# Three kept square sums on TensorE, two row slots, a second accumulator for the modulation columns, and another PSUM order: one change to a two-layer hybrid kernel

## The chip, the cores and the metric

The kernel runs on one core of one Trainium2 chip. The metric is device time in microseconds (us) of one execution. Engines are called by the names of the profile: PE (TensorE matmul), PEld (its weight load), DVE (VectorE), ACT (ScalarE), POOL (GpSimd), SP (SyncE, which here only issues DMAs).

## The reference, cut to what matters

Two layers run over 640 tokens (128 of a prompt, 512 of a sample) of width 1024. Each layer is a mixer and a SwiGLU FFN, each behind an RMSNorm whose scale and shift ("modulation") are products of two condition vectors with a large matrix:

```
mod  = silu(cond) @ ada_w[l] + ada_b[l]          # two conds (prompt, sample), 1024 x 6144 per layer
h    = rmsnorm(x, norm_mix_g[l]) * (1 + sc) + sh
x    = x + g * mixer_l(h)       # l=0: 4 mLSTM heads and 4 HGRN2 heads; l=1: differential attention, 8 heads
h    = rmsnorm(x, norm_ffn_g[l]) * (1 + sc2) + sh2
x    = x + g2 * (silu(h @ w1[l]) * (h @ w3[l])) @ w2[l]
y    = rmsnorm(x, final_norm_g)                  # behind the second layer
```

`rmsnorm` needs, of each token, the sum of 1024 squares. The mLSTM is chunkwise: of each head and each chunk of 128 tokens a 128x128 decay matrix (forward and backward) is made of row and column values, exponentiated and multiplied into the scores. The second layer's attention has a scalar `lam` made from `od_lambda`.

## The kernel before, in words

x lies feature-major, [128, 8, 640]: 8 blocks of 128 features, 640 tokens in the free dimension, worked in two halves a=0 and a=1 of 320 columns. Every fp32 product is three matmuls over split operands (high x high, low x high, high x low), all recorded at L188; transposes are at L193. Weights are loaded as 128x1024 fp32 (`raw`), and split into `wh` (ACT L318) and `wl` (DVE L319).

Order: a scheduler with its own timeline orders the instructions of ACT, DVE, POOL and SP; the order of PE is pinned as written in the mixers and in the transitions.

**Mixer of layer 0.** Eight units u (4 mLSTM heads `ml_mix`, u=0..3, then 4 HGRN2 heads `hg_mix`, u=4..7, `H4` = 4) run one after the other; a pacer (`Fill`) pulls the weight projections of the next unit into the steps of the present one. Beside them run side generators. In u=0..3 these are four units of `ada_vec` (L477 on): each makes 512 columns of modulation values without PE. It takes an accumulator `acc` (tag `qp`, one buffer), then 8 times loads a 128x512 piece `araw` (256 KB, two buffers in tag `fb`), scales it on ACT once for each of the two conditions (L486, into `acc` the first time, into `atmp` afterwards) and adds it on POOL (L488); at the end 4 PE matmuls `pj<-acc,ones` sum over the partitions. `add_side(..., 1)` lets one unit be loaded ahead of the unit that is being finished, and at `u == H4` a loop forces all that is left:

```
        if u == H4:
            while fill.side:
                fill.step_side()
```

In `ml_mix` each chunk makes `dm` = min(`nb`, `caus`) on DVE (L960), exponentiates it on ACT (L964), multiplies it with the scores and so on; `nb` holds rows of `nmd` from DRAM, broadcast to all partitions by `rows_of` (SP), in 5 slots of tag `kr`, loaded one head ahead.

**Transitions.** `transition()` stands three times: layer 0 mixer to FFN (T1), layer 0 FFN to attention (T2), attention to the last FFN (T3). Each adds the last products to x (`add_x`, DVE L371, 8 blocks of half 0, then of half 1), and has for each half: `sq_sum` (ACT L530 squares 8 blocks; 5 adds at L532 gather blocks 0 to 5 in `sq`, on POOL for half 0 and on DVE for half 1; DVE adds block 7 to block 6 at L534 and this to `sq` at L535), `columns` (5 matmuls `mean,sq` that put the means into 5 columns of 64 rows; DVE r L598; POOL power -0.5 L599; DVE dg L601), and `spread` (2 matmuls `dg,ones` that broadcast the result). Behind that, `norm_out` makes hh and hl on DVE and ACT (L548 to L570) and the next projection starts. Where in PE's order columns and spread stand is set by the tables BEFORE and BEHIND. In T2 the kernel also loads `lp` (`od_lambda`, SP L1590) and makes `nl` from it: DVE l2 L1593, DVE ls L1595, ACT exp L1596, DVE nl L1598.

**PSUM.** Pools of 8 banks are opened anew at each stage. `to_odd` opens one with tags pj, s and p1 for the second mixer, in place of a pool with pj (6 banks) and nm (2); a tag gets its banks when it is first used.

Of the kernel before, what the change touches and what calls it, by code (L numbers as in the profile page):

```python
# [9 lines left out]
F32 = mybir.dt.float32  # L10
F32R = mybir.dt.float32r
AF = mybir.ActivationFunctionType
ALU = mybir.AluOpType
# [3 lines left out]
P = 128  # L17
D = 1024
KD = D // P
NS = 512  # L20
NT = P + NS
NCH = NT // P
# [142 lines left out]
def hybrid_kernel(ctx: ExitStack, tc: tile.TileContext, A: dict, O: dict):  # L165
# [357 lines left out]
    def sq_sum(pool, a):  # L523

        t = slice(a * HALF, (a + 1) * HALF)
        sq = pool.tile([P, HALF], F32, tag="nsq", name="sq", bufs=2)
        s2 = pool.tile([P, HALF], F32, tag="ns2", name="s2", bufs=1)
        for k in range(KD):
            dst = {0: sq, SQUARES: s2}.get(k) or pool.tile([P, HALF], F32, tag="ns1", name="s1", bufs=2)
            S.activation(dst, x[:, k, t], AF.Square)  # L530
            if 0 < k < SQUARES:
                (V if a else G).tensor_tensor(sq, sq, dst, op=ALU.add)  # L532
            elif k > SQUARES:
                V.tensor_tensor(s2, s2, dst, op=ALU.add)  # L534
        V.tensor_tensor(sq, sq, s2, op=ALU.add)  # L535
        return sq

    def norm_out(pool, l, which, a, rs, ks=range(KD), keep=None):

# [44 lines left out]
    def transition(l, which, add, tag0, switch, tag1, nada, ada_bank, extra=0):  # L584
# [7 lines left out]
        def columns(sq, tag):  # L592

            o = bank(tag)
            for i in range(NC64):
                T.matmul(o[0:64, i:i + 1], lhsT=sq[:, i * 64:(i + 1) * 64], rhs=mean1, start=True, stop=True)
            r = pool.tile([64, NC64], F32, tag="nr", name="r", bufs=2)
            V.tensor_scalar(r, o[0:64, 0:NC64], EPS, None, op0=ALU.add)  # L598
            G.tensor_tensor(r, r, mhalf[0:64, 0:NC64], op=ALU.pow)  # L599
            dg = pool.tile([64, NC64, 64], F32, tag="ndg", name="dg", bufs=1)  # L600
            V.tensor_tensor(dg, ident[0:64, 0:64].unsqueeze(1).to_broadcast([64, NC64, 64]),  # L601
                            r.unsqueeze(2).to_broadcast([64, NC64, 64]), op=ALU.mult)
            return dg
# [306 lines left out]

        return (q, kf, so), [w_proj(c_q + h * P, evac_q), w_proj(c_k + h * P, evac_k), gen]

    nb = ev.tile([P, NCH, 2, P], F32, tag="kr", name="nb", bufs=1)

    def rows_of(h, c):

        Q.dma_start(nb[:, c], nmd[h, c:c + 1].to_broadcast([P, 2, P]))

    def ml_mix(h, q, kf, so):

# [34 lines left out]
        def weights(c):  # L955
            t = slice(c * P, (c + 1) * P)
            ps = p1()
            T.matmul(ps[:, 0:P], lhsT=kf[:, t], rhs=q[:, t], start=True, stop=True)
            dm = ev.tile([P, 2, P], F32, tag="dm", name="dm", bufs=2)
            V.tensor_tensor(dm, nb[:, c], caus, op=ALU.min)  # L960
            if h + 1 < H4:
                rows_of(h + 1, c)
            for r in range(2):
                S.activation(dm[:, r], dm[:, r], AF.Exp, bias=cols1[:, c, r, h:h + 1])  # L964
            V.tensor_tensor(dm, dm, ps[:, 0:P].unsqueeze(1).to_broadcast([P, 2, P]), op=ALU.mult)
            return dm
# [44 lines left out]

        mix["last"] = last

    for c in range(NCH):
        rows_of(0, c)


    def hg_bounds():
# [202 lines left out]
    for u, (_, mixer, h) in enumerate(units):  # L1221
        cur = nxt
        for p in HG_VALUES[u]:
            for g in hg_values(p):
                fill.add(g)
                val = g
        if u + 1 < len(units):
            nxt, gens = units[u + 1][0](units[u + 1][2])
            for g in gens:
                fill.add(g)  # L1230
        if u:
            fill.drain(key)
        key = gens[-1]
        for i in ADDS[u]:
            fill.add(add_gen(i))
        total = (48 * len(gens) if u + 1 < len(units) else 0) + 94 * len(HG_VALUES[u]) + 96 * len(ADDS[u])
        total += 48 if u == 0 else 0
        if u == 0:
            def acc():
                return ev.tile([P, 2, NT], F32, tag="qp", name="acc", bufs=1)[:, :, 0:512]  # L1240

            def raw():
                return ev.tile([P, NT], F32, tag="fb", name="araw", bufs=2)[:, 0:512]

            def tmp():
                return ev.tile([P, NT], F32, tag="kc", name="atmp", bufs=2)[:, 0:512]

            fill.add_side([ada_vec_gen(*i, raw, tmp, acc) for i in vec_units(VEC0)], VEC_EVERY, 1, eager=False)
        if u == H4:
            while fill.side:  # L1250
                fill.step_side()
        n, todo = ADA_UNITS[u], ada_todo[:ADA_UNITS[u]]
        del ada_todo[:n]
        if n:
            fill.add_side([ada_gen(j) for j in todo], total / (n + 0.5 - (2 if u == 7 else 0)))
        if u == 0:
            fill.pull(FILL0)
            total -= FILL0 * total / (total + 9 * n)
        quota = FRACTION[u] * (total + 9 * n) / (10 if u < H4 else 16)
        for step, w in enumerate(mixer(h, *cur)):  # L1260
            if u == H4 and step == len(LEVELS) + 1:
                fill.drain(val)
            fill.pull(w * quota)
            if last and step == LAST_STEP[u >= H4]:
                last()
                last = None
        last = mix["last"]
        if u == 3:
            ps = p1()
            T.transpose(ps[0:8, 0:P], nout.rearrange("p r h -> p (r h)"), ident)  # L1270
            nrow = ev.tile([8, P], F32, name="nrow")
            V.tensor_copy(nrow, ps[0:8, 0:P])
            Q.dma_start(O["mlstm_n"][0, 0].rearrange("r h d -> (r h) d"), nrow)
# [271 lines left out]
    def to_odd(behind):  # L1545
        ff["st"]["wide"].release()
        ff["st"]["pool"].release()
        psum["p"].release()
        psum_pool(pj=2, s=2, p1=2)
        ff["od"] = tc.alloc_tile_pool(name="od", bufs=1, reuse_waits="tile")  # L1550
        qk[0] = at_tiles()
        ws = [w_cols(w_in1, j * D, "r") for j in range(2)]
        with tc.issue_after(behind):
            wv = w_cols(w_in1, 2 * D)
        ff["vt"] = vt_tile()

        def first(a, between):
            os, t = proj_open(ws, a, between)
            for j in range(2):
                at_evac(j, qk[0][j], a, os[j], t)  # L1560
            (o,), t = proj_open([wv], a, lambda k: between(k + KD), [bank("s", 2)[:, 0:HALF]])
            S.copy(ff["vt"][:, t], o)

        return first
# [262 lines left out]
    def to_output():  # L1827
        ff["st"]["wide"].release()
        with tc.tile_pool(name="fi", bufs=1, reuse_waits="tile") as fi:
# [13 lines left out]
            def chunk(c):  # L1843
                o = bank("nm")
                for a in range(2):
                    t0, t1 = max(c * P, a * HALF), min((c + 1) * P, (a + 1) * HALF)
                    if t0 < t1:
                        T.matmul(o[t0 - c * P:t1 - c * P, 0:1], lhsT=sqs[a][:, t0 - a * HALF:t1 - a * HALF],
                                 rhs=mean1, start=True, stop=True)
                V.tensor_scalar(rcol[:, c:c + 1], o[:, 0:1], EPS, None, op0=ALU.add)  # L1850
                G.tensor_tensor(rcol[:, c:c + 1], rcol[:, c:c + 1], mhalf[:, 0:1], op=ALU.pow)
                for b in range(2):
# [58 lines left out]
```

## Time and profile before

| | us |
|---|---|
| median of 3 runs (lowest, highest) | 1824.48 (1822.47, 1824.6) |
| the profiled execution's own time | 1827.93 |
| its span in the trace | 1826.1 |
| PE busy in it | 1739.6 |

PE is busy 95% of the span, and its mean granted clock is 0.983 of full speed. Times of the trace run from the span's start; 1.8 us of the profiled execution lie outside the span. The mLSTM units of the first mixer lie at about 85 to 250 us, T1 at 487 to 515, T2 at 978 to 1015, T3 at 1355 to 1372, and the final norm behind 1806.

### The profile page before, as it was taken

How to read it: one execution, taken by the hardware profiler on the slowest of the kernel's cores; microseconds unless marked ns; L12 is line 12 of the kernel's file. 1: busy time of each engine (PE TensorE's matmuls, PEld its weight loads, DVE VectorE, ACT ScalarE, POOL GpSimd, SP SyncE). 2: the span in 40 equal slices, each digit the busy share in tenths (PEclk: the TensorE clock that was granted, in tenths of full speed). 3: DMA queues.
4: the chain of work that ended last, by engine and by line, in shares of the span. 5: the costliest groups of instructions: out<-in, count | busy, mean ns of one | idle time of the engine just before them, and what ended most of it. 6: DMA issues, size and time to landing. Idle time of an engine off the chain costs nothing.

```text
span 1826.1 us, 31627 instructions
## 1 busy us (share of the span) xinstructions
PE 1739.6 (95%) x12198; PEld 1661.5 (91%) x12198; DVE 1379.0 (76%) x2806; ACT 805.2 (44%) x1677; POOL 493.5 (27%) x409
## 2 busy tenths in 40 slices
PE   7998979999889999999999899999989999999998
PEld 5798969999778999999998898999978999999998
DVE  5657766677797777777778687777879887888787
ACT  5466543343353333333324466566536332333334
POOL 2244443233122222223211221112121333232321
PEclk9999989999989999999999999999999999999999
DMA  9344222122615434443412221112031322222211
GB/s 310 116 133 133 82 79 58 53 75 66 208 50 162 125 120 137 137 141 116 128 58 81 67 86 44 31 54 76 24 121 58 93 79 84 82 81 76 87 59 59
DMA packets 187979, 174.80 MB, mean 96 GB/s; under 512 B 7762, under 2 KB 168372, under 8 KB 187828
## 3 DMA queue, kind: packets, MB, share of 16 engines
q1 hardware_dynamic: 186564, 172.63, 30.7%
q8 instruction: 97, 1.59, 0.4%
q14 instruction: 54, 0.44, 0.1%
q10 hardware_dynamic: 1264, 0.14, 0.1%
HBM read 167.99 MB, written 4.74 MB: 95 GB/s over the span
## 4 chain that ended last, share of the span: by engine, by line
PE 76%; DVE 12%; DMA 4%; ACT 4%; issue 3%; POOL 1%; SPq 1%; ACTq 0%; DVEq 0%; POOLq 0%
PE pj L188 59%; PE nm L188 8%; PE p L188 5%; PE s L188 2%; DMA araw<-in_ada_w_dram 2%; DVE wl L319 2%; PE p L193 1%; DVE x L371 1%; ACT wh L318 1%; ACT atmp L486 1%; DVE hl L570 1%; DMA raw<-in_ffn_w_dram 1%; DMA wg<-in_ev_w_in_dram 0%; DVE hh L564 0%; PE pj L193 0%
## 5 line engine op out<-in xcount | busy, mean ns | idle before, releaser
L188 PE MATMUL pj<-hh,wh 128*128 128x320 f32 x1648 | 526.6, 322 | 11.9 <-DVE hh L564 5.7
L188 PE MATMUL pj<-hh,wl 128*128 128x320 f32 x1648 | 513.7, 312 | 0.0
L188 PE MATMUL pj<-hl,wh 128*128 128x320 f32 x1648 | 502.6, 313 | 2.1 <-DVE hl L570 1.9
L188 PEld LDWEIGHTS pj<-hh,wh 128*128 128x128 f32 x1648 | 313.1, 190 | 27.0 <-DVE hh L564 9.4
L188 PEld LDWEIGHTS pj<-hl,wh 128*128 128x128 f32 x1648 | 310.5, 190 | 3.9 <-DVE hl L570 2.4
L188 PEld LDWEIGHTS pj<-hh,wl 128*128 128x128 f32 x1648 | 313.8, 190 | 0.0
L188 PE MATMUL pj<-t,wh 128*128 128x320 f32 x960 | 217.0, 311 | 0.2 <-ACT wh L1322 0.2
L318 ACT CAST wh<-raw 128x1024 fp32r<-128x1024 f32 x127 | 132.6, 1048 | 184.8 <-PE pj L188 88.1
L319 DVE TENSOR_TENSOR wl<-raw,wh 128x1024 fp32r<-128x1024 f32 x127 | 162.8, 1284 | 40.0 <-ACT wh L318 39.7
L188 PEld LDWEIGHTS pj<-t,wh 128*128 128x128 f32 x960 | 160.9, 188 | 3.4 <-DVE o L1374 0.8
L1322 ACT CAST wh<-s 128x1024 fp32r<-128x1024 f32 x80 | 84.1, 1051 | 151.7 <-PE pj L188 151.7
L188 PE MATMUL pj<-t,wl 128*128 128x320 f32 x480 | 148.9, 310 | 1.1 <-DVE wl L1323 1.1
L1336 POOL TENSOR_TENSOR s<-raw 128x512 f32<-128x512 f32 x40 | 55.9, 1397 | 333.1 <-DVE wl L1323 331.5
L371 DVE SCALAR_TENSOR_TENSOR x<-nm,g2h,x 128x128 f32<-128x128 f32 (+1 forms) x236 | 93.5, 429 | 48.7 <-PE nm L188 48.3
L188 PE MATMUL pj<-ah,wh 128*128 128x320 f32 x392 | 122.5, 313 | 0.0
L188 PE MATMUL pj<-al,wh 128*128 128x320 f32 x392 | 121.3, 310 | 0.0
L188 PE MATMUL pj<-ah,wl 128*128 128x320 f32 x392 | 121.2, 309 | 0.0
L371 DVE SCALAR_TENSOR_TENSOR x<-pj,g2h,x 128x128 f32<-128x128 f32 (+2 forms) x292 | 112.1, 430 | 12.0 <-PE pj L188 11.3
L1338 POOL TENSOR_TENSOR s<-s,raw 128x512 f32<-128x512 f32 x40 | 66.4, 1659 | 198.3 <-DVE wl L1323 198.3
L1323 DVE TENSOR_TENSOR wl<-s,wh 128x1024 fp32r<-128x1024 f32 x80 | 97.2, 1215 | 8.5 <-ACT wh L1322 8.4
L1322 ACT CAST wh<-raw 128x512 fp32r<-128x512 f32 (+1 forms) x81 | 67.9, 838 | 80.1 <-PE pj L188 80.0
L188 PE MATMUL nm<-al,wh 128*128 128x320 f32 x312 | 96.3, 311 | 1.6 <-DVE al L1438 1.6
(415 smaller groups left out, 3898.4 us busy)
## 6 DMA issues: line engine op xcount, KB each, us to landing
raw<-in_ffn_w_dram SPq DMA_DIRECT2D x132, 512.0 KB
own<-in_ada_w_dram SPq DMA_DIRECT2D x48, 512.0 KB
raw<-in_ev_w_in_dram SPq DMA_DIRECT2D x36, 512.0 KB
raw<-in_od_w_in_dram SPq DMA_DIRECT2D x24, 512.0 KB
raw<-in_ada_w_dram SPq DMA_DIRECT2D x20, 512.0 KB
araw<-in_ada_w_dram SPq DMA_DIRECT2D x32, 256.0 KB
araw<-in_ada_w_dram SPq DMA_DIRECT2D x12, 512.0 KB
raw<-in_ev_w_out_dram SPq DMA_DIRECT2D x8, 512.0 KB
```

The source lines that it names most:

```text
L188: ins = nc.tensor.matmul(*args, **kw)
L193: ins = nc.tensor.transpose(*args, **kw)
L318: S.copy(wh, raw3)
L319: V.tensor_tensor(wl, raw3, wh.bitcast(F32), op=ALU.subtract)
L371: V.scalar_tensor_tensor(x[:, m, t0:t1], o[:, t0 - a * HALF:t1 - a * HALF], gate[:, m, c:c + 1], x[:, m, t0:t1], op0=ALU.mult, op1=ALU.add)
L486: S.activation(t, r, AF.Copy, scale=cpad[:, k, c:c + 1])
L570: order(V.tensor_tensor(hl[:, k, t], tmps[k], hh[:, k, t].bitcast(F32), op=ALU.subtract))
L1322: S.copy(wh, src)
L1323: V.tensor_tensor(wl, src, wh.bitcast(F32), op=ALU.subtract)
L1336: G.tensor_tensor(sa[:, 0], a21, a22, op=ALU.add)
L1338: G.tensor_tensor(sb[:, 0], sa[:, 0], a11, op=ALU.subtract)
```

## The change

Four edits stand in one diff. The sums: all five adds of both halves are on POOL, the two adds on DVE are gone, `sq_sum` hands over three parts, and `columns` (and the final `chunk`) sums them with three accumulating matmuls where there was one. The rows: `nb` has 2 slots in tag `sc` and a chunk's rows are loaded two chunks ahead. The modulation units: `acc` takes the tags `kr` and `qp` in turn, and two units may be ahead. The banks: `to_odd` takes both pairs of `s` banks first, so that s lies in the banks 0 to 3, pj in 4 and 5, p1 in 6 and 7, where pj lay in 0 and 1, p1 in 2 and 3 and s in 4 to 7.

```diff
@@ sq_sum
             if 0 < k < SQUARES:
-                (V if a else G).tensor_tensor(sq, sq, dst, op=ALU.add)
-            elif k > SQUARES:
-                V.tensor_tensor(s2, s2, dst, op=ALU.add)
-        V.tensor_tensor(sq, sq, s2, op=ALU.add)
-        return sq
+                G.tensor_tensor(sq, sq, dst, op=ALU.add)
+        return sq, s2, dst
@@ columns
             for i in range(NC64):
-                T.matmul(o[0:64, i:i + 1], lhsT=sq[:, i * 64:(i + 1) * 64], rhs=mean1, start=True, stop=True)
+                for j, part in enumerate(sq):
+                    T.matmul(o[0:64, i:i + 1], lhsT=part[:, i * 64:(i + 1) * 64], rhs=mean1, start=j == 0, stop=j == 2)
@@ rows
-    nb = ev.tile([P, NCH, 2, P], F32, tag="kr", name="nb", bufs=1)
+    nb = tt("sc", 1)[:, 0:4 * P].rearrange("p (i r t) -> p i r t", i=2, r=2)
-    def rows_of(h, c):
+    def rows_of(i):
-        Q.dma_start(nb[:, c], nmd[h, c:c + 1].to_broadcast([P, 2, P]))
+        h, c = divmod(i, NCH)
+        Q.dma_start(nb[:, i % 2], nmd[h, c:c + 1].to_broadcast([P, 2, P]))
@@ ml_mix
-            V.tensor_tensor(dm, nb[:, c], caus, op=ALU.min)
-            if h + 1 < H4:
-                rows_of(h + 1, c)
+            i = h * NCH + c
+            V.tensor_tensor(dm, nb[:, i % 2], caus, op=ALU.min)
+            if i + 2 < H4 * NCH:
+                rows_of(i + 2)
@@ modulation units
+            accs = [0]
+
             def acc():
-                return ev.tile([P, 2, NT], F32, tag="qp", name="acc", bufs=1)[:, :, 0:512]
+                accs[0] += 1
+                a = ev.tile([P, 2, NT], F32, tag=("qp", "kr")[accs[0] % 2], name="acc", bufs=1)
+                return a[:, :, 0:512]
-            fill.add_side([ada_vec_gen(*i, raw, tmp, acc) for i in vec_units(VEC0)], VEC_EVERY, 1, eager=False)
+            fill.add_side([ada_vec_gen(*i, raw, tmp, acc) for i in vec_units(VEC0)], VEC_EVERY, 2, eager=False)
@@ to_odd
+        vs = [bank("s", 2)[:, 0:HALF] for _ in range(2)]
-            (o,), t = proj_open([wv], a, lambda k: between(k + KD), [bank("s", 2)[:, 0:HALF]])
+            (o,), t = proj_open([wv], a, lambda k: between(k + KD), [vs[a]])
@@ chunk (final norm)
-                        T.matmul(o[t0 - c * P:t1 - c * P, 0:1], lhsT=sqs[a][:, t0 - a * HALF:t1 - a * HALF],
-                                 rhs=mean1, start=True, stop=True)
+                        for j, part in enumerate(sqs[a]):
+                            T.matmul(o[t0 - c * P:t1 - c * P, 0:1], lhsT=part[:, t0 - a * HALF:t1 - a * HALF],
+                                     rhs=mean1, start=j == 0, stop=j == 2)
```

Line numbers of the changed kernel differ by a few from those of before (L979 stays, L601 becomes L599, L1593 becomes L1599). On PE the order stays, but for the 10 further matmuls of each columns. On the other engines the order moves at three places.

The first is ACT, in the mLSTM phase, where the first `ada_vec` unit has just ended (`dm`, `inter`, `dn`, `hs` belong to the chunks, `k<-pj` and `so<-pj` are evacuations of projections, `atmp<-araw` is the modulation unit). Before:

```order
L964 ACTIVATE dm<-dm,cols_87 128x128
L990 ACTIVATE junk,ss<-hs 128x128
L486 ACTIVATE atmp<-araw,cpad 128x512 x2
L979 ACTIVATE inter<-p_1340,cols_87 128x129 x2
L964 ACTIVATE dm<-dm,cols_87 128x128 x2
L318 CAST wh<-raw 128x1024
L909 COPY k<-pj 128x320
L984 ACTIVATE dn<-inter 128x2
L979 ACTIVATE inter<-p_1391,cols_87 128x129 x2
```

Of the change, at the same place:

```order
L990 ACTIVATE junk,ss<-hs 128x128
L486 ACTIVATE atmp<-araw,cpad 128x512 x3
L979 ACTIVATE inter<-p_1398,cols_87 128x129 x2
L964 ACTIVATE dm<-dm,cols_87 128x128 x2
L318 CAST wh<-raw 128x1024
L486 ACTIVATE atmp<-araw,cpad 128x512
L907 COPY k<-pj 128x320
L984 ACTIVATE dn<-inter 128x2
L486 ACTIVATE atmp<-araw,cpad 128x512 x2
L979 ACTIVATE inter<-p_1449,cols_87 128x129 x2
```

The second unit's work has moved up into chunks that had none. In the same way the third unit now stands where the second stood (134 to 165 us of the trace before), the fourth where the third stood (185 to 208), and the stretch in which the fourth stood (225 to 263) has none.

The second place is POOL in T1 (`s<-raw` are POOL's own share of preparing FFN weights, `r<-r,mhalf` is the power of columns, `sq<-sq,s` the adds). Before:

```order
L1337 TENSOR_TENSOR s<-raw 128x512
L599 TENSOR_TENSOR r<-r,mhalf 64x5
L1336 TENSOR_TENSOR s<-raw 128x512
L1338 TENSOR_TENSOR s<-s,raw 128x512
L1339 TENSOR_TENSOR s<-raw,s 128x512
```

Of the change:

```order
L532 TENSOR_TENSOR sq<-sq,s_5665 128x320
L1341 TENSOR_TENSOR s<-raw 128x512
L532 TENSOR_TENSOR sq<-sq,s_5668 128x320
L597 TENSOR_TENSOR r<-r,mhalf 64x5
L1340 TENSOR_TENSOR s<-raw 128x512
L532 TENSOR_TENSOR sq<-sq,s_5671 128x320
L1342 TENSOR_TENSOR s<-s,raw 128x512
L532 TENSOR_TENSOR sq<-sq,s_5674 128x320
L1343 TENSOR_TENSOR s<-raw,s 128x512
```

The five adds of half 1 stand between the weight instructions, and two of them stand ahead of the first power.

The third place is DVE in T2, ahead of half 1's norm (`l<-lp`, `ls` and `nl` are the attention's scalar, `r` and `dg` belong to columns, `wl`, `hl` and `h` to weights and to the norm). Before:

```order
L319 TENSOR_TENSOR wl<-raw,wh 128x1024 x2
L570 TENSOR_TENSOR hl<-hf,hh 128x320
L534 TENSOR_TENSOR s_10876<-s_10876,s_10894 128x320
L570 TENSOR_TENSOR hl<-hf,hh 128x320
L535 TENSOR_TENSOR sq<-sq,s_10876 128x320
L598 TENSOR_SCALAR r<-p_10964 64x5
L1593 TENSOR_TENSOR l_11144<-lp 1x128
L1595 TENSOR_REDUCE ls<-l_11144 1x2
L601 TENSOR_TENSOR dg<-ident,r 64x320
L1598 SCALAR_TENSOR_TENSOR nl<-ls 1x1
L548 TENSOR_TENSOR h_10991<-x,p_10989 128x320 x2
```

Of the change:

```order
L319 TENSOR_TENSOR wl<-raw,wh 128x1024
L567 TENSOR_TENSOR hl<-hf,hh 128x320
L1599 TENSOR_TENSOR l_11176<-lp 1x128
L1601 TENSOR_REDUCE ls<-l_11176 1x2
L1604 SCALAR_TENSOR_TENSOR nl<-ls 1x1
L596 TENSOR_SCALAR r<-p_10988 64x5
L599 TENSOR_TENSOR dg<-ident,r 64x320
L545 TENSOR_TENSOR h_11025<-x,p_11023 128x320 x2
```

The two adds are gone, and r, which stood ahead of the first instruction that needs `lp`, now stands behind all three.

## Rows read from the trace of the kernel before

**Rows 1.** The page, parts 1 and 2: busy time; granted clock in 40 slices.

```profile
PE 1739.6 (95%) x12198; PEld 1661.5 (91%) x12198; DVE 1379.0 (76%) x2806; ACT 805.2 (44%) x1677; POOL 493.5 (27%) x409
...
PEclk9999989999989999999999999999999999999999
```

**Rows 2.** Busy time by stretch: stretch, length, PE, PEld, DVE, ACT, POOL, clock, DMA, GB/s.

```profile
108.00:134.00 26.00, 24.48 (x168) 22.79 (x167) 18.34 (x52) 14.74 (x47) 4.59 (x7) 1.00 0.41 119
134.00:165.00 31.00, 25.17 (x174) 24.12 (x173) 27.27 (x48) 20.65 (x48) 20.87 (x17) 1.00 0.45 136
...
185.00:208.00 23.00, 22.47 (x154) 21.91 (x153) 19.58 (x44) 15.08 (x35) 18.46 (x14) 1.00 0.38 115
208.00:246.50 38.50, 38.50 (x270) 36.98 (x268) 29.02 (x65) 20.28 (x52) 10.75 (x11) 1.00 0.23 69
246.50:267.00 20.50, 8.31 (x37) 6.21 (x37) 13.92 (x21) 9.26 (x24) 13.20 (x11) 0.58 0.33 97
267.00:300.00 33.00, 33.00 (x265) 33.00 (x265) 21.58 (x49) 10.99 (x23) 10.62 (x12) 1.00 0.17 49
```

**Rows 3.** PE in time, end of the mLSTM phase: start, us, operation, idle before.

```profile
249.17 0.27 PE L193 MATMUL p<-ident,nout 128*8 128x128 f32 x1 [2.64 <-issue]
...
261.62 1.07 PE L188 MATMUL pj<-acc,ones 128*32 128x256 f32 x4 [9.40 <-POOL acc L488]
```

**Rows 4.** The chain that ended last, 225 to 270 us.

```profile
by line: DMA araw<-in_ada_w_dram 51.7%; ACT atmp L486 19.5%; PE pj L188 15.5%; POOL acc L488 4.0%; ACT acc L486 3.0%; DVE kc L1094 2.7%; DVE hs L987 2.4%; issue 1.8%; DVE dn L985 1.6%; DVE hs L988 0.8%; ACT junk L990 0.6%; PE pj L193 0.5%; 
...
255.62 3.29 DMA araw<-in_ada_w_dram
```

**Rows 5.** The tiles acc and atmp, whole run: ns lowest/median/highest.

```profile
L488 POOL TENSOR_TENSOR acc<-acc,atmp x56: 1257/1287/2279, 89.5 to 261.5; 128x512 f32<-128x512 f32 x56
...
L486 ACT ACTIVATE atmp<-araw,cpad x56: 705/720/752, 88.7 to 259.6; 128x512 f32<-128x512 f32 x56
```

**Rows 6.** In time, T1, POOL and DVE.

```profile
491.45 4.68 POOL L532 TENSOR_TENSOR sq<-sq,s 128x320 f32<-128x320 f32 x5 [13.19 <-ACT s L530]
501.25 1.29 POOL L1337 TENSOR_TENSOR s<-raw 128x512 f32<-128x512 f32 x1 [5.12 <-DMA raw<-in_ffn_w_dram]
...
500.59 0.48 DVE L532 TENSOR_TENSOR sq<-sq,s 128x320 f32<-128x320 f32 x1
...
501.27 1.62 DVE L532 TENSOR_TENSOR sq<-sq,s 128x320 f32<-128x320 f32 x1
...
506.58 0.48 DVE L601 TENSOR_TENSOR dg<-ident,r 64x320 f32<-64x320 f32 x1
```

**Rows 7.** PE in time, T1.

```profile
500.35 0.71 PE L188 MATMUL pj<-mean,sq 128*64 128x1 f32 x10 [1.42 <-DVE sq L535]
...
507.21 0.77 PE L188 MATMUL pj<-dg,ones 64*128 64x320 f32 x2 [1.76 <-DVE dg L601]
```

**Rows 8.** PE in time, T2.

```profile
997.04 0.41 PE L188 MATMUL pj<-hh,wh 128*128 128x320 f32 x1 [2.33 <-DVE x L371]
...
1006.24 0.74 PE L188 MATMUL p<-mean,sq 128*64 128x1 f32 x10 [2.71 <-DVE sq L535]
...
1012.45 0.80 PE L188 MATMUL p<-dg,ones 64*128 64x320 f32 x2 [1.96 <-DVE dg L601]
```

**Rows 9.** In time, T2, SP, DVE and POOL.

```profile
1005.65 0.81 SPq L1590 DMA_DIRECT2D lp<-in_od_lambda_dram  x1
...
1007.02 0.15 DVE L598 TENSOR_SCALAR r<-p 64x5 f32<-64x5 f32 x1 [0.83 <-PE p L188]
1011.41 0.28 DVE L1593 TENSOR_TENSOR l<-lp 1x128 f32<-1x128 f32 x1 [4.23 <-DMA lp<-in_od_lambda_dram]
...
1011.93 0.47 DVE L601 TENSOR_TENSOR dg<-ident,r 64x320 f32<-64x320 f32 x1
...
1007.26 1.17 POOL L599 TENSOR_TENSOR r<-r,mhalf 64x5 f32<-64x5 f32 x1 [19.33 <-DVE r L598]
```

**Rows 10.** PE in time, T3.

```profile
1367.11 1.43 PE L188 MATMUL p<-dg,ones 64*128 64x320 f32 x2 [1.51 <-DVE dg L601]
```

More of the change, by code (lines that the diff above doesn't have):

```diff
@@ L1012, in ml_mix @@
         mix["last"] = last
-    for c in range(NCH):
-        rows_of(0, c)
+    for i in range(2):
+        rows_of(i)
     def hg_bounds():
```

## The prediction

> **What bounds the kernel now.** I read the page first: PE is busy 1739.6 of 1826.1 us, so at most 86 us can come from waits, and the sixth of its 40 slices shows a lower clock [rows 1]. Then I cut the mixer into stretches, and one stands out: between 246.5 and 267 us PE is busy 8.31 of 20.5 us at a granted clock of 0.58, while the stretches on both sides have no idle time and a clock of 1.00 [rows 2]. PE's own order of time says what it waits for there: 2.64 us ahead of a transpose and 9.40 us for POOL's `acc`, the end of the fourth modulation unit, which the loop at `H4` forces [rows 3]. The chain of waits between 225 and 270 us is 51.7% the loads `araw` and 19.5% ACT's `atmp`: loads and scalings take turns, since the unit works with one `araw` slot while the other `fb` slot is held by the first HGRN2 head [rows 4]. So the biggest single stall is the fourth unit, late. The other waits that the change touches are small: in the transitions PE waits 1.42 and 1.76 us in T1 [rows 7], 2.33, 2.71 and 1.96 us in T2 [rows 8] and 1.51 us in T3 [rows 10], each on DVE.
>
> **The change, part by part.**
>
> *The modulation units.* Each unit stands one place earlier, and nothing stands at 225 to 263 us. What does the stretch 246.5 to 267 need without a stall? Its 37 matmul records cost, by its neighbours, 33.00/265 = 0.125 to 38.50/270 = 0.143 us each [rows 2], so 4.6 to 5.3 us; 20.5 less that is 15.2 to 15.9 us. I take **-15.6**. The low bound of the gain is the two waits alone, 12.0 us [rows 3], if the clock fell for some other reason. That the clock was halved because PE had just stood still is what the rows suggest, since it is 1.00 ahead of it and behind it.
>
> What is paid for it: the second unit now stands in 108 to 134 us. A unit is 16 scalings of 0.72 us and 14 adds of 1.29 us [rows 5], 11.5 us of ACT and 18 of POOL. That stretch had 14.74 us of ACT in 26, so ACT would have 26.2: it is full, and part of the unit runs over into what follows. In the three stretches 108 to 134, 134 to 165 and 185 to 208 together, however, ACT was busy 14.74 + 20.65 + 15.08 = 50.5 us of 80 [rows 2], and has 62 after the move, so the overrun finds room. Units in other places cost PE 31.00 - 25.17 = 5.8 us (134 to 165) and 23.00 - 22.47 = 0.5 us (185 to 208), and the empty stretch has 1.5 us of idle time of its own [rows 2]. Third and fourth unit merely take over these two places. For the second I take the mean of both, **+3**, bounds +0 and +13; the high bound is ACT at the share that it reached in stretches with a unit, 20.65/31 = 0.67, for which 26.2 us of work need 39 us, 13 more than there are.
>
> *The rows' slots* are the same 20 transfers. They are asked for two chunks ahead, and 20 chunks lie between about 85 and 250 us, some 8 us each, so I cost them at nothing; the cover is that lead of some 16 us, against 2 to 4 us that a load of the modulation unit takes in the chain [rows 4]. If a row came late, DVE would stand at `dm`, and ACT's exponentials and the next chunk's matmuls with it; one us late in each of 20 chunks would be +20, which I keep as a thing to look for, not in the range.
>
> *The sums.* A columns costs 0.71 us of PE, 10 records for its 5 matmuls [rows 7]. With 15 matmuls it costs three times that, **+1.4** each, in 6 places. PE is in order, so this is on the path wherever PE doesn't wait anyway just ahead of or behind it. Removed from DVE are 7 instructions of half 1 and 2 of half 0, about 0.48 each, and on POOL appear 5 of 4.68/5 = 0.94 [rows 6].
>
> T1: columns waits 1.42 us for DVE's L535 [rows 7]. That add is gone and so is most of the wait, against +1.4. Spread waits 1.76 us for dg, and dg stood at 506.58 behind DVE's adds, one of which took 1.62 us beside POOL's L1337 instead of 0.48 [rows 6]. Without these, dg comes 1 to 2 us earlier; but by the new order of POOL two adds and a weight instruction precede its power, +1. The second columns is +1.4 again, beside DVE's norm work, which is itself waited for and gets 2.4 us of adds less. Sum **-0.5**, bounds -3 and +2.
>
> T2: the first wait, 2.33 us, is of a projection whose bank the old pool's sums still use; the new bank order puts other banks first, so it can go [rows 8]. The second, 2.71 us for L535, can go too. What sets the end is spread: it waits 1.96 us for dg. Now dg needs r, r stands behind nl on DVE, and nl needs `lp`, which landed at 1011.4, 5.8 us after its issue at 1005.65, with DVE waiting 4.23 us [rows 9]. Before, r and POOL's power (1007.02, 1007.26) were done by then, and dg started at 1011.93. After, it is l2 0.28 and about as much for ls, the exp and nl each, then r 0.15, power 1.17 and the steps between, some 2.8 us behind 1011.41, so dg at 1014.2 instead of 1011.93: +2.2. `lp` itself is issued behind weight loads, whose slots DVE frees: the first columns moves it by +1.4, DVE's missing adds by -2, their meeting with POOL's by up to +1.5; +0.8. What is gained at the first two waits only lengthens the third. Sum **+3**, bounds 0 (`lp` 3 us earlier) and +5.
>
> T3: spread waits 1.51 us for dg, which stood between DVE's adds [rows 10]. With none of them there it goes, and two columns cost +2.8, of which the second lies under the norm. Sum **-0.7**, bounds -2.5 and +1. Final norm: five chunks with 12 more matmuls in all, at 0.14 each by a columns' 5 in 0.71 us [rows 7], 1.7 us, most behind the last additions to x: **+0.4**, 0 to +1.
>
> **A rule that speaks against it.** DVE's add at 501.27 took 1.62 us, started 0.02 us behind POOL's 1.29 us instruction, where the add at 500.59 took 0.48 [rows 6]: the two engines hold each other up. So 15 adds that move to POOL also have 15 times 0.94 us in which they can hold DVE, against 15 that no longer are held themselves. The Trainium skill, page "SBUF — State Buffer", section "Who interferes with whom", says that DVE with two SBUF inputs and a GpSimd instruction that reads SBUF share one port pair, locked by the first for its whole instruction; by this rule the adds hold DVE on POOL just as POOL's other work did, and the trace agrees in the 1.62 us. My sum nets this to nothing; the case against is a rival.
>
> **Sum.** -15.6 + 3 - 0.5 + 3 - 0.7 + 0.4 = -10.4. The profiled execution took 1827.93 us, 3.45 above the median; its sum is 1817.5. Taken from the median, 1824.48 - 10.4 = **1814**.
>
> **Rivals.**
> *The moved work holds up others.* Either the second unit costs nearly its high bound, or the adds on POOL cost half of their 14 us on DVE's path: -10.4 + 5 to 9, so 1819 to 1823, about 1820. For it: ACT's 26.2 us of 26 and the 1.62 us. Against it: ACT has 18 us free in the three stretches, and the third unit's place costs 0.5 us.
> *The stall stays (slower).* The fourth unit, at 185 to 208 us, must be done when the loop at `H4` runs. It has 246 - 208 = 38 us to spare. If crowding pushes each of units 2 to 4 back by some 13 us, its end lies at 246, and beyond that PE stands still as before. Then the 15.6 are not gained, and the rest, +3 -0.5 +3 -0.7 +0.4 = +5.2, gives 1830. It decides from a delay of 38 us; the whole price comes at some 53, when the unit ends as late as now, at 261, and below 52 what is saved already brings the time under 1828. For it: the 31 us that the second unit took against the third's 23 [rows 2]. Against: these are 8 us between crowded and free, and not 38.
> *Part of the edit does nothing.* The wait at 261.62 goes, but another work of the first HGRN2 head comes too late and PE waits in the same place; half the gain, 1822.
>
> **Chances.** The forecast 0.68, with its own range 1808 to 1820; better than that 0.05; the moved work 0.12, half of it under the limit of faster; half the gain 0.08; the stall stays or another slowdown 0.07. 0.2%, 3.6 us, is about what a measurement of this kernel can tell from no change: faster is under 1820.9, slower above 1828.1. Faster 0.68 + 0.05 + 0.06 + 0.03 = 0.82, same 0.11, slower 0.07. The range 1806 to 1822 leaves out about 0.15.
>
> **What would show it.** In the profile of the changed kernel, 246 to 267 us should have no idle time on PE and a clock of 1.00, and the last `acc` adds should end near 208. Between 108 and 134 us ACT should be near full, with PE idle for 2 to 7 us. In T2, spread should wait for dg behind `lp`, 3 to 4 us. A columns should take about 2.1 us. Wrong would be: `acc` still added at 240 us or later; waits at `dm` for rows; or a T2 whose wait grows past 8 us.

## The result, and the profile after

| | us |
|---|---|
| before, median of 6 runs | 1824.1 (1822.47 to 1825.78) |
| after, median of 6 runs | 1837.4 (1832.45 to 1841.5) |
| ratio after to before, 95% interval | 1.0059 (1.0042 to 1.0076) |
| after, profiled execution and its span | 1838.05, 1836.2 |

The changed kernel is slower by 0.6% by the ratio, 13.3 us by the medians, where 10 us less were forecast. The first row of the page, for the changed kernel:

```profile
PE 1756.0 (96%) x12342; PEld 1678.8 (91%) x12342; DVE 1358.5 (74%) x2770; ACT 805.2 (44%) x1677; POOL 511.9 (28%) x429
```

The span grew by 10.1 us, and none of this is idle time of PE: it is busy 16.4 us more than before (1739.6 [rows 1]) and idle 6.3 us less, 80.2 us for 86.5. So the loss shows as more matmuls (144 more records) and as slower ones, at a lower granted clock, and not as longer waits in sum. The mean granted clock of its six runs is 0.980 to 0.986; in the runs of the kernel before that stand beside the experiments it is 0.982 to 0.988.

The stretch that was to be won was won. Busy time by stretch, of the changed kernel, with the columns of [rows 2]:

```profile
108.00:134.00 26.00, 21.16 (x136) 20.08 (x136) 20.04 (x40) 18.11 (x46) 17.49 (x15) 0.96 0.48 141
134.00:165.00 31.00, 22.26 (x121) 20.84 (x120) 19.83 (x42) 18.90 (x43) 19.64 (x16) 0.78 0.39 116
...
185.00:208.00 23.00, 23.00 (x165) 22.07 (x164) 17.46 (x39) 13.72 (x30) 8.34 (x7) 1.00 0.34 92
...
246.50:267.00 20.50, 18.63 (x131) 17.56 (x130) 11.39 (x29) 7.44 (x23) 3.32 (x3) 0.95 0.26 71
```

Between 246.5 and 267 us PE is now busy 18.63 us at a clock of 0.95, where it was 8.31 at 0.58 [rows 2], and the last `acc` add begins at 217.3 instead of 261.5. But in 108 to 165 us PE is busy 43.4 us where it was 49.65 [rows 2], and the clock there fell to 0.96 and 0.78. What PE waited for, of the changed kernel in time:

```profile
115.58 0.67 PE L188 MATMUL p<-cs,q 128*128 128x258 f32 x2 [1.20 <-DVE cs L951]
129.19 0.66 PE L193 MATMUL p<-ident,k 128*128 128x128 f32 x4 [1.91 <-ACT inter L979]
131.58 0.33 PE L193 MATMUL p<-ident,k 128*128 128x128 f32 x1 [1.73 <-DVE inter L981]
147.23 1.33 PE L193 MATMUL p<-ident,hs 128*128 128x128 f32 x5 [5.52 <-DVE hs L866]
```

PE waits for the chunks' small steps (`inter` for ACT too), and those are late on DVE and POOL. DVE and POOL in time, of the changed kernel:

```profile
110.72 0.41 DVE L960 TENSOR_TENSOR dm<-sc,caus 128x256 f32<-128x256 f32 x1
111.06 0.15 DVE L985 TENSOR_TENSOR dn<-dn,cols 128x2 f32<-128x2 f32 x1
...
120.76 1.25 DVE L985 TENSOR_TENSOR dn<-dn,cols 128x2 f32<-128x2 f32 x1
...
122.13 1.40 DVE L960 TENSOR_TENSOR dm<-sc,caus 128x256 f32<-128x256 f32 x1
...
145.30 1.88 DVE L866 TENSOR_TENSOR hs<-hs,rst 128x640 f32<-128x640 f32 x1 [3.02 <-POOL rst L687]
```

```profile
120.29 4.39 POOL L488 TENSOR_TENSOR acc<-acc,atmp 128x512 f32<-128x512 f32 x3 [0.98 <-ACT atmp L486]
...
142.86 1.26 POOL L488 TENSOR_TENSOR acc<-acc,atmp 128x512 f32<-128x512 f32 x1 [2.76 <-ACT atmp L486]
144.08 1.19 POOL L687 TENSOR_TENSOR rst<-rst,mhalf 128x5 f32<-128x5 f32 x1
```

Two things are to be seen. An add of two columns took 1.25 us instead of 0.15 and a min 1.40 instead of 0.41 while POOL's three adds ran back to back. And the head norm's power, `rst`, ready for POOL at 142.3, stands behind an add that itself waits 2.76 us for ACT; `hs` waits for it, and PE 5.52 us for `hs`.

In the second transition the new order of DVE cost time, as forecast. PE, DVE and SP in time, of the changed kernel:

```profile
1016.69 1.43 PE L188 MATMUL p<-dg,ones 64*128 64x320 f32 x2 [7.01 <-DVE dg L599]
...
1013.78 0.28 DVE L1599 TENSOR_TENSOR l<-lp 1x128 f32<-1x128 f32 x1 [5.14 <-DMA lp<-in_od_lambda_dram]
...
1014.71 0.14 DVE L596 TENSOR_SCALAR r<-p 64x5 f32<-64x5 f32 x1
1016.15 0.48 DVE L599 TENSOR_TENSOR dg<-ident,r 64x320 f32<-64x320 f32 x1 [1.29 <-POOL r L597]
...
1009.31 0.30 SPq L1596 DMA_DIRECT2D lp<-in_od_lambda_dram  x1
```

The wait for dg grew from 1.96 to 7.01 us [rows 8], because r starts behind `lp`, which came 2.4 us later than before [rows 9].

To place differences I lined up the DVE and ACT instructions that both traces have equally often, and took the median difference of their starts around fixed places of the trace before (80, 210, 300, 480, 530, 970, 1030, 1340, 1395 and 1800 us). The differences between neighbouring places say how much a stretch became longer or shorter. Each row is one profiled execution against that of before, whose time was itself 3.45 us over the median. Its own luck is in it: most traces are 0.1 to 2.2 us shorter than that of before between 530 and 970 us, where nothing was changed, so a us or two in "other" or a transition means nothing.

| us, against before | to 210 | 210-300 | T1 | T2 | T3 | end | other | span |
|---|---|---|---|---|---|---|---|---|
| the change | +11.1 | -12.7 | +2.0 | +4.4 | +1.3 | +2.7 | +1.2 | +10.1 |
| e1 units and rows | +10.4 | -12.5 | -0.6 | -0.3 | -3.3 | +0.5 | -1.6 | -7.3 |
| e2 sums | +0.9 | +1.0 | +5.7 | +2.8 | +2.3 | +3.2 | -0.5 | +15.4 |
| e4 change, lp early | +11.5 | -13.6 | +5.0 | -3.7 | +1.8 | +2.9 | -1.0 | +2.9 |
| e6 units, adds out | +4.9 | -12.3 | -1.3 | +0.1 | -1.1 | -0.1 | +0.3 | -9.6 |
| e7 spaced units | +8.3 | -15.2 | +4.1 | -2.4 | -2.7 | -0.2 | -0.8 | -8.9 |
| e8 parts | +0.5 | -2.0 | -1.0 | -0.4 | -2.2 | +1.9 | -1.9 | -5.0 |
| e11 spaced, p1 | +9.3 | -15.2 | +0.0 | -3.2 | -3.2 | +0.7 | +0.8 | -10.6 |
| e13 sums, lp early | +0.5 | -0.1 | +1.3 | -3.1 | +4.9 | +1.9 | +1.6 | +7.0 |
| e14 sums, adds out | +0.6 | -0.7 | -1.3 | +2.8 | -1.4 | +1.9 | -1.9 | 0.0 |

So in these traces the mixer gained 12.7 us and gave back 11.1, and the places of the sums lost the rest.

### The profile page after: what moved, and what is told of

Same layout as the page of the kernel before. It is cut to its first block, busy times and chain, and to the rows that moved or that the text cites. A ratio compares the mean times of both kernels' runs of the same rounds, so it can differ in the third digit from the quotient of the medians.

```text
span 1836.2 us, 31896 instructions
## 1 busy us (share of the span) xinstructions
PE 1756.0 (96%) x12342; PEld 1678.8 (91%) x12342; DVE 1358.5 (74%) x2770; ACT 805.2 (44%) x1677; POOL 511.9 (28%) x429
## 5 line engine op out<-in xcount | busy, mean ns | idle before, releaser
L188 PEld LDWEIGHTS pj<-hh,wh 128*128 128x128 f32 x1648 | 314.2, 191 | 26.3 <-DVE hh L561 12.5
L371 DVE SCALAR_TENSOR_TENSOR x<-pj,g2h,x 128x128 f32<-128x128 f32 (+2 forms) x292 | 112.0, 431 | 16.1 <-PE pj L188 15.4
```

Of the source, the lines that this page charges most:

```text
L188: ins = nc.tensor.matmul(*args, **kw)
L371: V.scalar_tensor_tensor(x[:, m, t0:t1], o[:, t0 - a * HALF:t1 - a * HALF], gate[:, m, c:c + 1], x[:, m, t0:t1], op0=ALU.mult, op1=ALU.add)
```

## The experiments

Times are medians; the ratio is to runs of the kernel before on the same chip, with its 95% interval.

**e1_units: the modulation units and the rows' slots alone** (the hunks "rows", "ml_mix" and "modulation units" of the change).

> The kernel before with the rows' slots and the modulation units of the change, without its sums and its bank order. Theory (the second unit crowds 108 to 165 us and gives back there what the fourth unit's stall cost): the mixer gains and loses about 12 us each, so the median stays within 4 us of the kernel before, with no idle time at 246 to 267 us and PE some 11 us later at 165 us. Rival (the losses come from the sums alone, and the crowding seen in one profile was chance): 8 to 13 us faster than before.

1821.13 us against 1823.83, ratio 0.9986 (0.9977 to 0.9995). The theory held: in the trace 12.5 us gained, 10.4 given back ahead of 210 us. The rival is out. By itself this part is a small gain.

**e2_sums: the sums alone** (the hunks "sq_sum", "columns" and "chunk").

> The kernel before with the sums of the change alone. Theory (columns of 15 matmuls and r behind lp are the price of the change outside the mixer): 6 to 10 us slower than before, of it 2 to 3 in the first transition, 3 to 5 in the second, 1 to 2 in the third, 2 to 3 in the final norm, nothing in the mixer. Rival (the second transition's loss is the bank order's): 3 to 5 us slower, with the second transition within 1 us of before.

1840.17 us, ratio 1.0091 (1.0075 to 1.0108): 16 us, more than either side had. The whole loss of the change, and more, is here. Its first transition shows a DVE instruction of a length that the trace of before doesn't have. DVE, POOL and PE in time, of e2:

```profile
507.93 4.63 DVE L599 TENSOR_TENSOR dg<-ident,r 64x320 f32<-64x320 f32 x1
...
506.86 1.27 POOL L1334 TENSOR_TENSOR s<-raw 128x512 f32<-128x512 f32 x1
508.09 0.87 POOL L532 TENSOR_TENSOR sq<-sq,s 128x320 f32<-128x320 f32 x1
508.92 1.26 POOL L1336 TENSOR_TENSOR s<-s,raw 128x512 f32<-128x512 f32 x1
510.14 0.85 POOL L532 TENSOR_TENSOR sq<-sq,s 128x320 f32<-128x320 f32 x1
510.96 1.26 POOL L1337 TENSOR_TENSOR s<-raw,s 128x512 f32<-128x512 f32 x1
...
512.71 1.40 PE L188 MATMUL pj<-dg,ones 64*128 64x320 f32 x2 [3.87 <-DVE g2h L472]
```

dg, 0.48 us elsewhere [rows 6], took 4.63 us: it began while POOL ran, and ended just behind the last of five POOL instructions that followed one another without a gap, at 512.2. PE waited 3.87 us for it (the view names the short DVE instruction just behind dg), 1.76 before [rows 7]. In the kernel before, the two engines took turns at this place; DVE and POOL in time, of before:

```profile
504.00 1.52 DVE L532 TENSOR_TENSOR sq<-sq,s 128x320 f32<-128x320 f32 x1
...
503.90 1.27 POOL L1336 TENSOR_TENSOR s<-raw 128x512 f32<-128x512 f32 x1
505.25 1.39 POOL L1338 TENSOR_TENSOR s<-s,raw 128x512 f32<-128x512 f32 x1
```

There DVE's add ended 0.35 us behind the end of one POOL instruction; the next began 0.08 us behind that end, and took 1.39 us instead of 1.27. In e2 the moved adds fill such gaps between the weight instructions, and dg stays out until the row of five ends. That this happens every time is not shown: in the first transition of the changed kernel and of e13, with the same adds on POOL, dg took 0.48 us, and in e4 it took 1.55 and came through behind one POOL instruction though POOL had no gap there.

**e3_banks: the bank order alone** (the hunk "to_odd").

> The kernel before with the other order of the banks alone. Theory: the wait of 2.33 us in the second transition goes, but spread still waits for dg behind lp, so 0 to 2 us faster, within the noise. Rival (the bank order lengthens the second transition): 2 to 5 us slower.

1824.49 us, ratio 1.0005 (0.9994 to 1.0016). No change; the rival is out. In its trace the wait of 2.33 us is gone, no wait in its place is longer than 0.74, but the next one, for sq ahead of columns, grew from 2.71 [rows 8] to 4.41 us.

**e4_lp_early: the change, lp and nl ahead of the first FFN.**

```diff
+    lp = sm.tile([P, NB * P], F32, tag="adasb", name="lp", bufs=2)[0:1, 0:256].rearrange("p (a d) -> p a d", a=4)
+    Q.dma_start(lp, A["od_lambda"])
...
     last = ffn_rest(ff["st"], ticker(vec, ADA_TICK))
...
-    lp = od.tile([1, 4, 64], F32, name="lp")
-    Q.dma_start(lp, A["od_lambda"])
```

> The changed kernel with lp loaded and nl computed before the first layer's FFN, so that r and dg of the second transition no longer stand behind that load. Theory (lp holds r and dg): the wait of 7.0 us for dg falls under 2 us and the time falls by 4 to 7 us against the changed kernel, to about 1831. Rival (dg is late for another reason, the POOL's adds or the squares): it falls by less than 2 us.

1833.49 us, ratio 1.0063 (1.0047 to 1.008). PE in time, of e4:

```profile
1009.65 1.43 PE L188 MATMUL p<-dg,ones 64*128 64x320 f32 x2 [0.29 <-DVE dg L599]
```

The wait for dg fell from 7.01 to 0.29 us and T2 from +4.4 to -3.7, so r behind lp does hold dg there. Whether the time fell is not shown: the median is 3.9 us below that of the change, but the ratio to before is no better than that of the change (1.0059). T1 was 3 us longer in this trace, and e15 below shows that the edit has a price of its own.

**e5_one_ahead: e1 with one unit ahead.**

```diff
-VEC_EVERY, 2, eager=False)
+VEC_EVERY, 1, eager=False)
```

> As e1, but with one unit ahead instead of two: the second unit stands early (it has its own accumulator), the fourth stays where it was. Theory (the early second unit alone costs some 9 to 11 us): the fourth unit's stall stays and the time is 7 to 13 us over the kernel before, with PE behind by 8 to 12 us at 210 us. Rival (the crowding needs both units ahead, loads of the third included): within 4 us of before.

1833.77 us, ratio 1.0059 (1.0044 to 1.0074), 9.6 us over before. The second unit still moved up, since it has its own accumulator, and the fourth stayed. The time is what the theory had: this is the price of the early unit without the gain. Its second sign, PE behind by 8 to 12 us at 210 us, is missing: in the one trace it is 5.7 us.

**e6_no_adds: e1 without most of the second unit's adds on POOL** (that unit's values are not summed).

```diff
-                if k:
+                if k and (l or j != 20 or k == KD - 1):
                     G.tensor_tensor(a[:, c], a[:, c], t, op=ALU.add)
```

> As e1, but 12 of the second unit's 14 adds on POOL are left out (its modulation values are not summed); its loads and ACT's scalings stay. Theory (POOL's adds hold DVE's small steps and POOL's own power of the head norm): the loss up to 210 us falls from 9.4 us to under 4, and the time to about 1815. Rival (ACT is the one that is full, as the prediction's bound had it): the loss stays at 8 us or more.

1815.28 us, ratio 0.9954 (0.9938 to 0.997), 5.8 us below e1's median. The time is what the theory had. Up to 210 us 4.9 us are lost instead of 10.4, more than the theory's 4, though ACT still does all of its scalings; the rival is out. POOL's adds are thus a little over half of the price of the place. The rest was not divided: ACT, the loads and the third unit are left, and PE still waits 4.26 us for `hs` there.

**e7_spaced: the kernel before with the units spaced otherwise** (`VEC_EVERY` sets the distance of the units' steps).

```diff
-VEC0, VEC_EVERY = 4, 211
+VEC0, VEC_EVERY = 4, 165
```

> The kernel before with one number changed, VEC_EVERY 165 for 211: the four units keep one accumulator and one lead, but stand at about 92 to 119, 128 to 158, 175 to 199 and 208 to 225 us. Theory (the stall at 246 us is worth some 13 us, and it is only the place of the second unit that gave it back): 9 to 13 us faster than before, about 1812. Rival (any unit moved up costs what it gains): within 4 us of before.

1819.46 us, ratio 0.998 (0.9971 to 0.9989): 4.7 us faster, less than the theory wanted. The stall goes (-15.2), but even with these places 8.3 us are lost up to 210 us; the rival is half right. And T1 lost 4 us to a wait that before did not have. PE in time, of e7:

```profile
510.60 0.63 PE L188 MATMUL pj<-hh,wh 128*128 128x320 f32 x1 [6.96 <-DVE hf L548]
```

**e8_parts: three parts on TensorE, half 1's adds on DVE** (the hunks "columns" and "chunk" of the change, and this).

```diff
                 (V if a else G).tensor_tensor(sq, sq, dst, op=ALU.add)
-            elif k > SQUARES:
-                V.tensor_tensor(s2, s2, dst, op=ALU.add)
-        V.tensor_tensor(sq, sq, s2, op=ALU.add)
-        return sq
+        return sq, s2, dst
```

> The kernel before with the three parts on TensorE, but with half 1's five adds left on DVE (its two last adds are gone). It tells the matmuls of columns from the move to POOL. Theory (10 more matmuls cost 1.2 us in each of 6 columns and some 2 to 3 us in the final norm, and the clock falls behind them; r stands behind lp here too): 8 to 14 us slower than before. Rival (the adds on POOL, which meet DVE, are the price): under 5 us slower.

1827.37 us, ratio 1.0019 (1.0009 to 1.0028): 3.2 us. The theory, for which the matmuls were the price, falls; the rival holds. The trace shows +1.9 us at the end, in the final norm. It also differs from e2 in DVE's order: r stands ahead of lp here, only l2 and ls stand ahead of dg, and PE waits 3.49 us for dg where it waits 4.69 in e2.

**e9_move: only the five adds to POOL.**

```diff
-                (V if a else G).tensor_tensor(sq, sq, dst, op=ALU.add)
+                G.tensor_tensor(sq, sq, dst, op=ALU.add)
```

> The kernel before with half 1's five adds on POOL and nothing else changed: columns keeps its 5 matmuls, DVE its two last adds. With e2 and e8 it divides the price of the sums. Theory (POOL's adds between its weight instructions are late themselves and hold DVE's two-operand instructions): 5 to 11 us slower than before, most of it in the first and third transitions and the final norm. Rival (the price of e2 is in the pair of both edits, r behind lp above all, which only the pair brings about): within 3 us of before.

1829.1 us against 1826.04, ratio 1.0021 (1.0009 to 1.0033). About 3 us: the rival's bound. Here r and dg stand ahead of lp on DVE, so the order that e2 got does not come about. Neither half of the sums alone explains 16 us, nor do both together: 3 and 3. Its first transition shows the long row a second time; DVE and PE in time, of e9:

```profile
504.02 2.04 DVE L472 TENSOR_TENSOR g2h<-adar,v 128x4 f32<-128x4 f32 x1
506.10 4.04 DVE L473 TENSOR_SCALAR g2h<-g2h 128x4 f32<-128x4 f32 x1
510.06 0.47 DVE L601 TENSOR_TENSOR dg<-ident,r 64x320 f32<-64x320 f32 x1
...
510.68 1.40 PE L188 MATMUL pj<-dg,ones 64*128 64x320 f32 x2 [6.27 <-DVE dg L601]
```

The instruction of 4.04 us, 0.15 in the trace of before, reads one SBUF operand, and ended as a gap-free row of POOL ended, at 510.1. dg stood behind it, and PE waited 6.27 us.

**e10_best: e7 and the early lp** (the edits of e7 and of e15).

> The kernel before with VEC_EVERY 165 and with lp loaded and nl computed ahead of the first FFN: the two edits that the runs speak for. Theory (both waits are separate): 5 to 9 us faster than before, about 1817, with the second transition 0 to 3 us shorter than before. Rival (before, lp does not hold dg by more than its two short instructions, so that edit brings nothing): 4 to 5 us faster, as e7.

1825.68 us against 1826.04, ratio 0.9994 (0.9981 to 1.0006): worse than e7, a miss for both. With the early lp added, what the spacing gave is gone.

**e11_spaced_p1: e7 with other banks in T1.**

```diff
-    transition(0, 1, add_open(w6, acts[6], mod[:, 0, 16:24]), "pj", to_ffn(0, 6, 2), "nm", ADA_TRANS[0], p1)
+    transition(0, 1, add_open(w6, acts[6], mod[:, 0, 16:24]), "p1", to_ffn(0, 6, 2), "nm", ADA_TRANS[0], pj)
```

> As e7, but in the first transition columns and spread take their banks from p1 and the modulation products theirs from pj. In e7 PE waited 6.96 us there, to the end of the last norm multiplication that reads the spread sums in a pj bank, which the new pool hands to the first projection. Theory (that bank is the wait): the first transition loses some 4 us of what it has in e7, and the time is about 1816, 7 to 10 us under the kernel before. Rival (DVE's work itself is late there): as e7, 4 to 5 us under.

1817.3 us against 1825.78, ratio 0.9957 (0.9945 to 0.997): 8.5 us faster than before. PE in time, of e11, the longest wait at that place:

```profile
508.62 0.41 PE L188 MATMUL pj<-hh,wh 128*128 128x320 f32 x1 [1.02 <-DVE hh L564]
```

The wait of 6.96 us is gone (T1 from +4.1 to 0.0). The banks of the two tags were the cause, as the theory had it; this is the fastest version found that computes everything, and it beats both kernels.

**e12_repair: the change with half 1's adds back on DVE and lp early.**

> The changed kernel with two edits taken back or mended: half 1's five adds on DVE again (three parts on TensorE stay), and lp loaded and nl computed ahead of the first FFN. Theory (adds on POOL and r behind lp are the 13 us by which e2 exceeds e8): what stays is the units' -2.7 and the parts' +3.2, so 1820 to 1828. Rival (the loss is spread over more, or the units lose more beside the other parts): 1830 or more.

1832.32 us against 1825.78, ratio 1.0031 (1.002 to 1.0042). Over the theory's 1820 to 1828; the rival won. With e15 the ratios add up after all: e1 -0.14%, e8 +0.19%, e3 +0.05%, e15 +0.22%, together +0.32%. The theory had left out the price of the early lp. Each of these has an interval of some 0.1% to either side.

**e13_sums_lp, e14_no_adds1, e15_lp_alone** divide the pair: the sums with lp early; the sums with half 1's five adds left out on every engine (its squares 1 to 5 are not summed); the kernel before with lp early. The edit of e14, against e2:

```diff
-            if 0 < k < SQUARES:
+            if 0 < k < SQUARES and not a:
                 G.tensor_tensor(sq, sq, dst, op=ALU.add)
```

> The sums alone (as e2) with lp loaded and nl computed ahead of the first FFN, so that r and dg of the second transition stand behind no load. Theory A (r behind lp is what both edits bring about only together): the time falls from e2's 16 us over before to 5 to 9 us over it. Theory B (POOL's adds, which hold DVE in the first and third transitions, are the larger part): it stays 11 us or more over before.

> The sums alone (as e2), with half 1's five adds left out on every engine (its squares 1 to 5 are not summed); three parts on TensorE and r behind lp stay. Theory A: still 9 us or more over before, since r waits for lp as in e2. Theory B: 2 to 6 us over before, near e8, where these adds are on DVE.

> The kernel before with lp loaded and nl computed ahead of the first FFN, the control for e10, e12 and e13. If that edit is free of other effects: 0 to 2 us faster than before. If it shifts the first transition, as the profiles of e10 and e12 suggest: 1 to 4 us slower.

e13: 1838.03 against 1825.77, ratio 1.0059 (1.0044 to 1.0075). e14: 1826.84, ratio 1.0006 (0.9994 to 1.0017). e15: 1829.9, ratio 1.0022 (1.0012 to 1.0032). Theory A falls with e14: r still stands behind lp there, PE still waits for it, and the time is 1 us over before. PE in time, of e14:

```profile
1010.13 1.43 PE L188 MATMUL p<-dg,ones 64*128 64x320 f32 x2 [5.32 <-DVE dg L599]
```

Theory B holds in the main: e13 stays 12.3 us over before by the medians, and without the adds on POOL 15 of e2's 16 us are gone, more than theory B had; with the adds on DVE (e8) 13. T1, T3 and the end are 7.0, 3.7 and 1.3 us shorter in e14's trace than in e2's, and T2 is the same. The first row of the page, of e2 and of e14:

```profile
PE 1753.8 (95%) x12342; PEld 1677.5 (91%) x12342; DVE 1362.9 (74%) x2770; ACT 806.4 (44%) x1677; POOL 510.7 (28%) x429
...
PE 1746.7 (96%) x12342; PEld 1669.1 (91%) x12342; DVE 1357.2 (74%) x2770; ACT 805.7 (44%) x1677; POOL 495.1 (27%) x409
```

The spans are 1841.5 and 1826.1 us, so of the 15.4 us between the two 8.3 are idle time of PE and 7.1 are longer busy time for the same 12342 records. The clock agrees: the means of e2's runs are 0.980 to 0.983, those of e14's 0.982 to 0.989, of e8's 0.984 to 0.990 and of the kernel before beside e2 0.984 to 0.988. Taking lp away (e13) is worth 0.32% beside the adds, or 0.54% if the edit's own 0.22% is put to it, so the two prices overlap, and their sum is more than the whole. Where the early lp itself loses its 4 us is open: its trace shows 0.3 us in T1 and 0.6 at the end, and was 1.3 us longer in all.

## Why the prediction was wrong, by its steps

**The stall: right.** The step "-15.6" measured -12.3 to -15.2 in the traces, -12.7 in the change, near its low bound of 12.0. Between 246.5 and 267 us PE is nearly busy and at full clock, 18.63 of 20.5 us at 0.95, as the prediction said. The kernel is slower all the same, to which the prediction gave 0.07, mostly for a stall that stays; it did not stay.

**The second unit: the mechanism was right, the size wrong.** The term was +3, from the mean of two places with a unit, with +13 as a bound; from 80 to 210 us it measured 9.4 us in e1 and 11.6 in the change. The argument that the overrun "finds room" counted ACT's busy time over three stretches. But a chunk is a chain of short steps that pass through ACT, DVE and POOL; by the rows of the change what counts is not whether the work finds room but how long a step stands behind a 0.72 us scaling or a 1.29 us add. e6 shows that POOL's adds are about half of it, which the sum had left without a price. The old place of the second unit, 5.8 us [rows 2], was the nearer row: it too had adds beside a chunk's chain, and a head's end with `hs` behind `rst`. The mean with the 0.5 us place pulled the value away from it, though 5.8 would have been some 4 us too low as well.

**The sums: the wrong step.** The sum of T1, T2, T3 and the final norm was +2.2 us; e2 measured 16. The step that failed is "My sum nets this to nothing": 15 adds that leave DVE against 15 that come to POOL. (With the final norm they are 20: POOL has 429 instructions for 409.) Where the adds are left out (e14) or on DVE (e8), 15 and 13 of the 16 us are gone, so beside the three parts the adds on POOL are not nothing but most of the price.

How they cost it is shown in part. To net out, a DVE instruction must lose no more to POOL than before, at most one instruction of POOL in the rows of before. In e2 dg, which PE waits for, was kept out by a row of five, 4.63 us, and in e9 the instruction ahead of dg for 4.04. The Trainium skill, page "SBUF — State Buffer", section "Who interferes with whom", which the prediction weighed, says that the lock holds for the whole instruction of whoever issued first; the trace agrees that dg, with two SBUF operands, waits beside POOL instructions that read SBUF, and goes beyond it in length: the wait passed over four boundaries between POOL instructions. But the changed kernel's own trace has no such row at its dg in T1. About half of what the adds cost is not in waits at all but in matmuls at a lower clock (7.1 of 15.4 us, e2 against e14, one trace each); what lowered the clock there was not tested. And the adds alone cost 3 us (e9) and the parts alone 3 (e8), so some 10 us come only with both. r behind lp, which only both bring about, is in it: T2 is +2.8 us in e2 and -3.1 in e13. Yet e14 keeps that order, and T2 at +2.8, at 1 us over before. What else ties the two halves stays open.

T1 and T3, forecast at -0.5 and -0.7, are +2.0 and +1.3 in the change's trace and +5.7 and +2.3 in e2's. The rival "the moved work holds up others" had the mechanism and set it at 5 to 9 us over the sum; with the second unit's it was about 20 (14 for the sums in e2, 6 for the unit in e1).

**A columns at +1.4 each:** 15 matmuls, 30 records, take 1.91 us in the first columns of the change, 0.71 before [rows 7]; +1.2, nearly right. Together with DVE's two missing adds the matmuls cost 3 us (e8), not the 8 of six columns at 1.4.

**T2: the mechanism was right, the size low.** Forecast +3 with lp as what sets the end; measured +4.4 in the change, with dg at 7.01 us of wait where 3 to 4 were forecast, and a clock that had fallen. e4 shows the wait gone with the early lp. **The final norm:** forecast +0.4 with a bound of +1, measured +2.7 (1.9 in e8). The clock is 0.61 in the last 10 us, 0.87 before, where PE is busy 5.16 us for 4.20; that the further matmuls lie on the path there is argued, not shown.

**Rows' slots and bank order** at nothing: e3 agrees for the banks. The rows were not run by themselves, only with the accumulators' tags; in the changed kernel no PE wait stands on their load.

## What to carry to other kernels

Work that is moved to an engine with free time costs by whom it keeps waiting, not by its busy time: look at what stands in a row there, and whether the one instruction that the matmuls wait for has to get past that row. Read the matmul engine's busy time beside its idle time: a loss can be whole in the first, through more matmuls and a lower clock. Price a move by the nearest place that has the same neighbours (5.8 us here), not by the mean of near and far ones. And try the cheapest way to a gain first: another spacing of the same units, one number, and another bank tag gave 8.5 us where four edits lost 13.

## What the runs showed of the hardware that was not expected

A DVE instruction can be kept out by several POOL instructions in a row: 4.63 us for one of 0.48 with two SBUF operands (e2), 4.04 us for one of 0.15 with one (e9). In other traces one came through behind the first (1.55 us, e4); what decides it is not shown.

PE's clock fell without PE standing still. Busy time by stretch in the second transition of the changed kernel:

```profile
984.00:988.00 4.00, 4.00 (x45) 3.72 (x43) 1.36 (x4) 0.00 (x0) 0.61 (x1) 1.00 0.00 0
988.00:992.00 4.00, 4.00 (x25) 2.53 (x24) 1.29 (x3) 0.84 (x2) 0.56 (x1) 0.57 0.46 132
992.00:996.00 4.00, 4.00 (x26) 3.56 (x26) 3.63 (x10) 3.38 (x9) 0.87 (x1) 1.00 0.45 134
```

PE was busy 4.00 of 4.00 us in each, and the granted clock went to 0.57, 1.2 GHz for most of the stretch, behind the 30 records of a columns with 1 column each (985.2 to 987.1), beside 16 records of `pj<-raw,cpad` from 988.1 on. The kernel before, with 10 records and the same 16 behind them, kept 1.00 there:

```profile
986.10:990.00 3.90, 3.90 (x32) 2.66 (x32) 2.44 (x6) 1.71 (x5) 1.72 (x3) 1.00 0.47 138
```

It does not happen every time. Three columns of each trace, the first in T2 and the second in T1 and T3, have no wait of PE right behind them. The clock fell behind them at 10 of the 21 such places in the traces of the seven kernels with 30 records, and at none of the 30 in those of the ten with 10. So part of the price of narrow matmuls can be paid by the wide ones behind them.
